# Remainders of expert weights on GpSimd in the second top-k, and another spread of the early expert blocks

## The chip, the cores and the metric

The kernel runs on one NeuronCore of a Trainium2 chip. A core has five engines with a queue of their own each: TensorE (PE, whose weight loads the profile shows apart as PEld), VectorE (DVE), ScalarE (ACT), GpSimd (POOL) and SyncE (SP, which only issues DMAs here). Each works its queue in order, and engines wait for one another by semaphores. The metric is the device time of one execution in microseconds, as the median of several runs.

## The reference

One layer of a hybrid encoder over 1024 tokens of 1024 numbers in float32: a norm, a projection into attention and recurrent parts, their mix, and then the PEER layer, which the change is about:

```
q      = (rmsnorm(h) @ w_query) as (T, 8 heads, 2 halves, 128)
s1, s2 = q[:, :, 0] . sub_keys_1,  q[:, :, 1] . sub_keys_2       # 128 scores each
v1, i1 = top_k(s1, 16);  v2, i2 = top_k(s2, 16)
sc, ci = top_k(v1[..., :, None] + v2[..., None, :], 16)          # the second top-k, of 256 sums
eid    = i1[ci // 16] * 128 + i2[ci % 16];  g = softmax(sc)
act    = gelu(expert_down[eid] . x)
out    = sum over 8 * 16 slots of g * act * expert_up[eid]       # out of 16384 experts
```

followed by a residual sum and a last norm.

## The kernel before, in words

**Two ways through the experts.** The first 3 blocks of 128 tokens fetch their experts' rows one slot at a time by indirect DMA (`gathered`, L875 to L916): 768 steps, each a gather issued on GpSimd (L879) and one long VectorE instruction (L896 or L906) that consumes the row. Five row buffers go round, so a gather waits until VectorE has consumed an earlier row. These steps are strewn through all later stages by `gather_steps`. The other 5 blocks (`ND` = 5, 640 tokens) go the dense way: for each of 128 expert blocks e of 128 experts the product of all their down vectors with all 640 tokens is formed (`down_all`), passed through a GELU, multiplied with a sparse weight matrix that comes from one-hots of the top-k's keys, and multiplied with the up vectors.

**float32 products.** A weight tile is split into a float32r part, cast by ScalarE (`hi`, L126), and the remainder, a subtraction (`lo`, L127). Three products follow each time (`mm3`, L158, L161, L162): hi*hi, hi*lo of the tokens, lo*hi. In `down_all` the tiles are named `draw` (as loaded), `dh`, `dl`; the third product (L162) is the first that needs `dl`. `dh` and `dl` have two buffers, each half an expert block (512 columns). A block is 48 matmuls of 320 columns.

**Early expert blocks.** Of the 128 down products, 71 are formed ahead of the up stage, while other engines prepare the dense weights. `early_downs(n)` adds n to a running sum and forms a block for each whole unit of it; results go to DRAM (`act_d`), all but one. It is called in three loops, with E_QRY / 16 per step of the second query projection (16 steps), E_TOPK / 5 per dense token block in the second top-k, E_OH / 40 per step of the one-hot stage (40 steps of 16 tokens), and after the last step for all that are left.

**The second top-k** (loop over b of 5 token blocks). Nearly all of it is VectorE work: candidate sums, maxima with their indices, softmax, and the keys of the 16 best from comparisons. Its results (`five`) are transposed on TensorE (`ptk`, L1090) one loop step later. No gather steps are added in it (G_TOPK = 0).

**The one-hot stage.** Each step makes three one-hot tiles for 16 tokens (two VectorE instructions, 16 on ScalarE), 48 small matmuls (L1160), and copies of their results to DRAM (`gw_d`); 168 gather steps are spread over it. Then the up stage loads these weights (`gw`), the stored GELUs (`ga`), and forms the remaining down products between the up products.

**The order of the work.** Nobody writes the queues by hand: a planner simulates the program in time and puts each engine's instructions in the order in which they could start, the earlier in the program first. So one-hots appear among the last top-ks, and where an instruction moves to another engine all queues are planned anew. `keep_in_program_order` pins an instruction against the other pinned ones of its engine: the first matmul of each early block, the long VectorE instructions of the gather steps.

Of the kernel before, what the change touches and what calls it, by code (L numbers as in the profile page):

```python
# [39 lines left out]
ND = NT - NG  # L40
# [11 lines left out]
G_UP = 2 * NG * SLOTS - (G_ATT + G_OUT + G_QRY + G_TOPK + G_OH)  # L52
B_OUT, B_CHAIN, B_TURN, B_QRY, B_TOPK = 0, 3, 8, 8, 12
A_STEPS, A_AHEAD, A_FILL, LRU_AT, WO_AT = 3, 4, 0.5, 0.7, 50
E_QRY, E_TOPK, E_OH = 8, 20, 40
TURN5 = 2
OH_LAST = 96
NORM_IN = ((0,), (1,), (2, 3))
# [45 lines left out]
def trunk(  # L104
# [6 lines left out]
    V, A, G, T = nc.vector, nc.scalar, nc.gpsimd, nc.tensor  # L111
# [12 lines left out]
    def split(src, hi, lo, eng=None):  # L124

        A.copy(hi, src)  # L126
        (eng or V).tensor_sub(lo, src, hi.bitcast(F32))  # L127
# [28 lines left out]
    def mm3(ps, wh, wl, mh, ml, first, last, pin=False):  # L156

        t = T.matmul(ps, wh, mh, start=first, stop=False)  # L158
        if pin:
            tc.keep_in_program_order(t)  # L160
        T.matmul(ps, wh, ml, start=False, stop=False)  # L161
        T.matmul(ps, wl, mh, start=False, stop=last)  # L162
# [183 lines left out]
    pin = False  # L346
# [417 lines left out]
    with tc.tile_pool(name="at_gk", bufs=2, side="right") as at_k, \  # L764
# [47 lines left out]
        pin = True  # L812
# [108 lines left out]
    def gather_steps(n):  # L921

        due[0] += n
        while due[0] >= 1.0 - 1e-6:
            due[0] -= 1.0
            next(steps, None)
# [49 lines left out]
    with tc.tile_pool(name="op_d", bufs=1) as op, \  # L976
            tc.tile_pool(name="ps_od", bufs=3, space=PSUM) as ps_a:
        def turn(i, hg, diag):
            for q in range(2):
                pt = ps_t.tile([P, 4, P], F32, name="pt")  # L980
                sl = (slice(None), slice(4 * q, 4 * q + 4), slice(i * P, (i + 1) * P))
                for j in range(4):
                    t = T.matmul(pt[:, j, :], hg[:, (4 * q + j) * P:(4 * q + j + 1) * P], diag,
                                 start=True, stop=True)
                    if j == 0:
                        tc.keep_in_program_order(t)
                split(pt, xH[sl], xL[sl])
# [36 lines left out]
    dp = ctx.enter_context(tc.tile_pool(name="dp", bufs=2))  # L1024
    ps_d = ctx.enter_context(tc.tile_pool(name="ps_d", bufs=3, space=PSUM))

    def down_all(e, pin=False):

        ga = dp.tile([P, TD], F32, name="ga", bufs=2 + HOLD + PRE)
        pd = [ps_d.tile([P, 512], F32, name="pd") for _ in range(2)]  # L1030
        raw = dp.tile([P, KD, P], F32, name="draw", bufs=RAWS)
        nc.sync.dma_start(raw, down_t[e])
        for kh in range(2):
            wh = dp.tile([P, 4, P], F32R, name="dh")
            wl = dp.tile([P, 4, P], F32R, name="dl")
            split(raw[:, 4 * kh:4 * kh + 4, :], wh, wl)
            for c in range(2):
                sl = slice(c * HT, (c + 1) * HT)
                for k in range(4):
                    mm3(pd[c][:, :HT], wh[:, k, :], wl[:, k, :], xH[:, 4 * kh + k, sl],  # L1040
                        xL[:, 4 * kh + k, sl], kh == 0 and k == 0, kh == 1 and k == 3,
                        pin and kh == 0 and c == 0 and k == 0)
        for c in range(2):
            A.activation(ga[:, c * HT:(c + 1) * HT], pd[c][:, :HT], AF.Gelu_apprx_tanh)
        return ga
# [7 lines left out]
    with ExitStack() as ph:  # L1053
        todo = iter(early)
        left = [0.0]

        def early_downs(n):
            left[0] += n
            while left[0] >= 1.0 - 1e-6:
                left[0] -= 1.0  # L1060
                e = next(todo, None)
                if e is None:
                    return
                ga = down_all(e, pin=True)
                if e < HOLD:
                    made[e] = ga
                    continue
                act_d[e] = dram.tile([P, TD], F32, name=f"act{e}")
                nc.scalar.dma_start(act_d[e], ga)
# [4 lines left out]
        with tc.tile_pool(name="qp_d", bufs=3) as qp, \  # L1074
                tc.tile_pool(name="ps_q", bufs=3, space=PSUM) as ps_m, \
                tc.tile_pool(name="ps_qs", bufs=2, space=PSUM) as ps_s:
            for ct, _ in enumerate(query(weights, xH, xL, ND, v12, i12, qp, ps_m, ps_s)):
                if ct in TOPK_AT:
                    top_k_g(1 + TOPK_AT.index(ct), tk, v12_g, i12_g)
                gather_steps(G_QRY / (2 * PH))  # L1080
                early_downs(E_QRY / (2 * PH))
# [13 lines left out]

        last = None
        for b in range(ND):
            early_downs(E_TOPK / ND)

            five = sl_pool.tile([P, 5, P], BF, name="five", bufs=2)  # L1100
            gate = tk.tile([P, PH, TOPK], F32, name="gate_d")
            top_k(v12[:, b], i12[:, b], tk, five[:, 1, :].rearrange("p (h r) -> p h r", h=PH),
                  five[:, 0, :].rearrange("p (h r) -> p h r", h=PH), gate)
            gate = gate.rearrange("p h r -> p (h r)")
            for i in range(2, 5):
                A.copy(five[:, i, :], gate)
                if i < 4:
                    V.tensor_sub(gate, gate, five[:, i, :])
            if last:
                turn(*last)  # L1110
            last = b, five
            gather_steps(G_TOPK / ND)
# [57 lines left out]
        for t0 in range(0, TD, TB):  # L1170
            now = one_hots(t0)
            if t0 == TURN5 * TB:
                turn(*last_five)
            early_downs(E_OH * TB / TD)
            if last:
                weights(*last)
            last = t0, *now
            gather_steps(G_OH * TB / (TD - OH_LAST) if t0 < TD - OH_LAST else 0)
# [6 lines left out]
    with ExitStack() as ph:  # L1185
# [7 lines left out]
        def weigh(e):  # L1193

            if e % EQ == 0:
                gws[e // EQ] = gw = gp.tile([P, TD // TG, EQ * TG], F32, name="gw")
                part, k = (gw_d[0], e) if e < E_FIRST else (gw_d[1], e - E_FIRST)
                nc.sync.dma_start(gw, part[:, :, k:k + EQ, :].rearrange("a p e t -> p a (e t)"))
            gw = gws[e // EQ]
            if e in made:  # L1200
                ga = made[e]
            elif e in act_d:
                ga = dp.tile([P, TD], F32, name="ga", bufs=2 + HOLD + PRE)
                nc.sync.dma_start(ga, act_d[e])
            else:
                ga = down_all(e)
            j = e % EQ
            gv = ga.rearrange("p (a t) -> p a t", t=TG)
            V.tensor_tensor(gv, gv, gw[:, :, j * TG:(j + 1) * TG], op=ALU.mult)
            wh = wp.tile([P, TD], F32R, name="w_h")  # L1210
            wl = wp.tile([P, TD], F32R, name="w_l")
            split(ga, wh, wl)
            ws[e] = (wh, wl)

        for e in range(EARLY, min(EG, EARLY + PRE)):
            made[e] = down_all(e, pin=True)
# [5 lines left out]
        for g in range(NK // EG):  # L1222
            for second in range(2):
# [5 lines left out]
                for j in range(EG):  # L1229
                    e = g * EG + j  # L1230
# [6 lines left out]
                    raw = raw2[:, j % 2, :]  # L1237
# [10 lines left out]
                    wh, wl = ws[e]  # L1248
# [7 lines left out]
                for b in range(ND if end else 0):  # L1256
                    bs = slice(b * P, (b + 1) * P)
                    for e, uh, ul in tail:
                        wh, wl = ws[e]
# [66 lines left out]
```

## Time and profile before

| what | us |
|---|---|
| median of 3 runs (2752.73 to 2758.27) | 2756.99 |
| the profiled execution | 2756.29 |
| its span, first to last instruction | 2754.5 |
| TensorE busy | 2626.9 |
| VectorE busy | 2276.4 |
| ScalarE busy | 1200.6 |
| GpSimd busy | 1042.8 |

Times in the views are microseconds from the start of the span. The second query projection with its early blocks runs from about 685 to 846, the second top-k from there to about 1005, the one-hot stage to about 1410, the up stage to the end. Matmuls are pipelined: each is shown with some 0.31 us for 320 columns but they start closer together, so their pace is read from their starts. An engine's idle time counts only where the work that ends last stands behind it.

### The profile page before, as it was taken

Reading aid. Unit: us, or ns where it says so; the run is one execution under the profiler, and the core shown is the slowest. Engines: PE = TensorE matmul, PEld = TensorE weight load, DVE = VectorE, ACT = ScalarE, POOL = GpSimd, SP = SyncE. Lnnn points to the kernel's source line nnn. Section 1 sums busy time; section 2 is a strip of 40 time slices with the busy share of each in tenths; the row PEclk is TensorE's granted clock in tenths of the full one; section 3 lists DMA queues with packets and bytes.
Section 4 is the critical chain, followed back from the end, with each engine's and each line's share of the span. In section 5 each row is a group of like instructions: output and inputs, shape, how many; then the busy total and the mean of one; then the engine's idle time right before and its main releaser. Section 6 shows DMA issues by size and latency. Waiting matters only on the chain.

```text
span 2754.5 us, 43406 instructions
## 1 busy us (share of the span) xinstructions
PE 2626.9 (95%) x15577; PEld 2323.2 (84%) x15577; DVE 2276.4 (83%) x4737; ACT 1200.6 (44%) x2551; POOL 1042.8 (38%) x850
## 2 busy tenths in 40 slices
PE   7989987889999899999999999999999999999996
PEld 6767965747999899999988888888888888888885
DVE  6565878877999978989967789888888888888897
ACT  5763436722324667888853223222223222222222
POOL 1000223353322015443323445444454545545563
PEclk9999988989999999999999999999999999999998
DMA  5446888877675249999999999999999999999986
GB/s 193 154 138 230 314 242 238 259 256 271 233 255 174 92 162 350 356 341 335 338 370 326 334 351 326 336 332 352 339 332 336 330 340 326 348 338 338 338 288 242
DMA packets 319273, 795.75 MB, mean 289 GB/s; under 512 B 26209, under 2 KB 126577, under 8 KB 316497
## 3 DMA queue, kind: packets, MB, share of 16 engines
q0 software_dynamic: 118128, 428.28, 44.2%
q1 hardware_dynamic: 184112, 297.97, 32.1%
q10 hardware_dynamic: 16816, 66.72, 6.0%
q8 instruction: 122, 2.00, 0.3%
q14 instruction: 95, 0.77, 0.1%
HBM read 690.77 MB, written 102.11 MB: 288 GB/s over the span
## 4 chain that ended last, share of the span: by engine, by line
PE 70%; issue 11%; DMA 9%; DVE 6%; POOL 2%; ACT 2%; SPq 0%; DVEq 0%; ACTq 0%; POOLq 0%
PE pu L158 9%; PE pu L161 9%; PE pu L162 9%; PE pd L162 8%; PE pd L158 8%; PE pd L161 8%; PE pg L1160 4%; PE pa L158 3%; PE pa L162 2%; PE pa L161 2%; POOL row L879 2%; DMA row<-in_expert_up,eid 2%; DMA row<-in_expert_down,eid 2%; DVE row L896 1%; PE pa L606 1%
## 5 line engine op out<-in xcount | busy, mean ns | idle before, releaser
L879 POOL DMA_INDIRECT row<-in_expert_up,eid x384 | 513.1, 1336 | 666.9 <-DVE accg L906 542.2
L879 POOL DMA_INDIRECT row<-in_expert_down,eid x384 | 487.9, 1271 | 631.0 <-DVE row L896 504.2
L158 PE MATMUL pd<-xdH,dh 128*128 128x320 f32 x2048 | 639.6, 313 | 6.0 <-ACT dh L126 3.8
L162 PE MATMUL pd<-xdH,dl 128*128 128x320 f32 x2048 | 631.3, 311 | 10.8 <-DVE dl L127 10.8
L161 PE MATMUL pd<-xdL,dh 128*128 128x320 f32 x2048 | 634.6, 310 | 0.0
L906 DVE SCALAR_TENSOR_TENSOR accg<-row,wg,accg 128x1024 f32<-128x1024 f32 x384 | 491.3, 1279 | 27.0 <-DMA row<-in_expert_up,eid 24.1
L161 PE MATMUL pu<-ul,w_h 128*128 128x512 f32 x1280 | 503.5, 393 | 2.5 <-DVE ul L127 2.5
L162 PE MATMUL pu<-uh,w_l 128*128 128x512 f32 x1280 | 499.6, 392 | 0.0
L896 DVE SCALAR_TENSOR_TENSOR row<-row,x2g 128x1024 f32<-128x1024 f32 x384 | 460.6, 1218 | 32.3 <-DMA row<-in_expert_down,eid 29.9
L162 PEld LDWEIGHTS pd<-xdH,dl 128*128 128x128 f32 x2048 | 385.4, 189 | 19.4 <-DVE dl L127 12.8
L158 PE MATMUL pu<-uh,w_h 128*128 128x512 f32 x1280 | 393.5, 394 | 8.3 <-DVE acc L1261 3.3
L158 PEld LDWEIGHTS pd<-xdH,dh 128*128 128x128 f32 x2048 | 387.0, 189 | 14.5 <-ACT dh L126 4.1
L161 PEld LDWEIGHTS pd<-xdL,dh 128*128 128x128 f32 x2048 | 386.8, 189 | 8.2
L126 ACT CAST uh<-uraw 128x512 fp32r<-128x512 f32 x256 | 157.9, 620 | 498.3 <-PE pu L162 397.5
L161 PEld LDWEIGHTS pu<-ul,w_h 128*128 128x128 f32 x1280 | 241.9, 189 | 50.3 <-DVE ul L127 3.7
L158 PEld LDWEIGHTS pu<-uh,w_h 128*128 128x128 f32 x1280 | 238.1, 189 | 52.5 <-issue 3.7
L162 PEld LDWEIGHTS pu<-uh,w_l 128*128 128x128 f32 x1280 | 241.3, 189 | 47.8
L126 ACT CAST dh<-draw 128x512 fp32r<-128x512 f32 x256 | 157.9, 618 | 241.5 <-PE pd L161 226.9
L127 DVE TENSOR_TENSOR ul<-uraw,uh 128x512 fp32r<-128x512 f32 x256 | 175.5, 687 | 77.6 <-ACT uh L126 76.7
L127 DVE TENSOR_TENSOR dl<-draw,dh 128x512 fp32r<-128x512 f32 x256 | 175.4, 687 | 67.3 <-ACT dh L126 65.2
L126 ACT CAST w_h<-ga 128x640 fp32r<-128x640 f32 x128 | 93.3, 729 | 243.1 <-PE pu L161 166.3
L1147 ACT ACTIVATE o1a<-o,slot_a 128x128 bf16<-128x128 bf16 x640 | 194.1, 428 | 1.8 <-DVE o L1136 1.8
(282 smaller groups left out, 4050.7 us busy)
## 6 DMA issues: line engine op xcount, KB each, us to landing
draw<-in_down_t SPq DMA_DIRECT2D x128, 512.0 KB, 7.0
uraw<-in_up_h SPq DMA_DIRECT2D x128, 512.0 KB, 7.2
gw<-gw_d SPq DMA_DIRECT2D x32, 1280.0 KB, 15.2
gw_d<-st ACTq DMA_DIRECT2D x20, 1536.0 KB, 10.4
act<-ga ACTq DMA_DIRECT2D x70, 320.0 KB, 4.9
ga<-act SPq DMA_DIRECT2D x70, 320.0 KB, 9.7
w_d<-w POOLq DMA_DIRECT2D x32, 512.0 KB, 5.1
w<-w_d SPq DMA_DIRECT2D x32, 512.0 KB, 5.5
```

Of the source, the lines that this page charges most:

```text
L126: A.copy(hi, src)
L127: (eng or V).tensor_sub(lo, src, hi.bitcast(F32))
L158: t = T.matmul(ps, wh, mh, start=first, stop=False)
L161: T.matmul(ps, wh, ml, start=False, stop=False)
L162: T.matmul(ps, wl, mh, start=False, stop=last)
L606: T.matmul(pss[:, t - t0, :], qt[:, t * P:(t + 1) * P], kt[:, ct % 2, :], start=True, stop=True)
L879: nc.gpsimd.indirect_dma_start(out=r, out_offset=None, in_=table, in_offset=bass.IndirectOffsetOnAxis(ap=eids[tb][:, s:s + 1], axis=0))
L896: tc.keep_in_program_order(V.scalar_tensor_tensor(r, r, 1.0, x2, op0=ALU.mult, op1=ALU.mult, accum_out=act[:, s:s + 1]))
L906: tc.keep_in_program_order(V.scalar_tensor_tensor(acc, r, w[:, s:s + 1], acc, op0=ALU.mult, op1=ALU.add))
L1147: A.activation(oa[:, g, :, j], o[:, g, 1, :, j], AF.Copy, scale=slot_a[b][:, tt + t:tt + t + 1])
L1160: T.matmul(ps[:, t - t4, :], o[:, g, 0, :, j], part[:, g, :, j], start=i == 0, stop=i == 2)
```

## The change

In the loop of the second top-k, `early_downs` is called with GpSimd as the engine that forms the remainders `dl` of the weights; in the other loops and in the up stage VectorE goes on forming them. The engine is handed on through `early_downs` and `down_all` to `split`, which could already take one. E_TOPK goes from 20 to 25 (5 and not 4 blocks per token block), E_OH from 40 to 36 (0.9 and not 1 per step). E_QRY stays at 8.

```
@@ -52,7 +52,7 @@
 G_UP = 2 * NG * SLOTS - (G_ATT + G_OUT + G_QRY + G_TOPK + G_OH)
 B_OUT, B_CHAIN, B_TURN, B_QRY, B_TOPK = 0, 3, 8, 8, 12
 A_STEPS, A_AHEAD, A_FILL, LRU_AT, WO_AT = 3, 4, 0.5, 0.7, 50
-E_QRY, E_TOPK, E_OH = 8, 20, 40
+E_QRY, E_TOPK, E_OH = 8, 25, 36
 TURN5 = 2
 OH_LAST = 96
 NORM_IN = ((0,), (1,), (2, 3))
@@ -1024,7 +1024,7 @@
     dp = ctx.enter_context(tc.tile_pool(name="dp", bufs=2))
     ps_d = ctx.enter_context(tc.tile_pool(name="ps_d", bufs=3, space=PSUM))
 
-    def down_all(e, pin=False):
+    def down_all(e, pin=False, eng=None):
 
         ga = dp.tile([P, TD], F32, name="ga", bufs=2 + HOLD + PRE)
         pd = [ps_d.tile([P, 512], F32, name="pd") for _ in range(2)]
@@ -1033,7 +1033,7 @@
         for kh in range(2):
             wh = dp.tile([P, 4, P], F32R, name="dh")
             wl = dp.tile([P, 4, P], F32R, name="dl")
-            split(raw[:, 4 * kh:4 * kh + 4, :], wh, wl)
+            split(raw[:, 4 * kh:4 * kh + 4, :], wh, wl, eng)
             for c in range(2):
                 sl = slice(c * HT, (c + 1) * HT)
                 for k in range(4):
@@ -1054,14 +1054,14 @@
         todo = iter(early)
         left = [0.0]
 
-        def early_downs(n):
+        def early_downs(n, eng=None):
             left[0] += n
             while left[0] >= 1.0 - 1e-6:
                 left[0] -= 1.0
                 e = next(todo, None)
                 if e is None:
                     return
-                ga = down_all(e, pin=True)
+                ga = down_all(e, pin=True, eng=eng)
                 if e < HOLD:
                     made[e] = ga
                     continue
@@ -1095,7 +1095,7 @@
 
         last = None
         for b in range(ND):
-            early_downs(E_TOPK / ND)
+            early_downs(E_TOPK / ND, G)
 
             five = sl_pool.tile([P, 5, P], BF, name="five", bufs=2)
             gate = tk.tile([P, PH, TOPK], F32, name="gate_d")
```

## Rows read from the trace of the kernel before

**Rows 1.** The page, busy time, share and instructions of each engine

```profile
PE 2626.9 (95%) x15577; PEld 2323.2 (84%) x15577; DVE 2276.4 (83%) x4737; ACT 1200.6 (44%) x2551; POOL 1042.8 (38%) x850
```

**Rows 2.** Table by stretch, core 0: PE, PEld, DVE, ACT, POOL busy; PEclk, DMA, GB/s

```profile
846.00:915.00 69.00, 58.90 (x395) 57.55 (x394) 68.97 (x352) 33.09 (x60) 12.97 (x9) 0.97 0.53 181
850.00:1010.00 160.00, 145.74 (x1009) 142.36 (x1008) 146.05 (x586) 95.04 (x190) 13.21 (x10) 0.97 0.39 132
1010.00:1410.00 400.00, 397.45 (x3812) 391.65 (x3810) 353.84 (x304) 336.17 (x918) 173.83 (x116) 1.00 0.92 339
1100.00:1125.00 25.00, 25.00 (x229) 24.70 (x229) 23.43 (x25) 22.59 (x66) 12.81 (x8) 1.00 0.99 371
```

**Rows 3.** Waits of TensorE from 846 to 1010: us, times, longest

```profile
PE ptk L1090 <- DVE cand L670: 6.2, 1, 6.2
PE pd L162 <- DVE dl L127: 5.9, 4, 2.3
PE pd L158 <- ACT ga L1044: 2.2, 2, 1.8
```

**Rows 4.** Timeline of TensorE: start, us, what, [idle before it, releaser]

```profile
853.60 0.31 PE L161 MATMUL pd<-xdL,dh 128*128 128x320 f32 x1
855.16 0.42 PE L162 MATMUL pd<-xdH,dl 128*128 128x320 f32 x1 [1.25 <-DVE dl L127]
...
914.71 0.47 PE L161 MATMUL pd<-xdL,dh 128*128 128x320 f32 x1
...
918.17 0.37 PE L162 MATMUL pd<-xdH,dl 128*128 128x320 f32 x1
```

**Rows 5.** Timeline of ScalarE, two casts of half a block

```profile
849.69 0.62 ACT L126 CAST dh<-draw 128x512 fp32r<-128x512 f32 x1 [2.80 <-PE pd L161]
...
853.21 0.62 ACT L126 CAST dh<-draw 128x512 fp32r<-128x512 f32 x1 [0.88 <-PE pd L161]
```

**Rows 6.** VectorE's instruction groups, 850 to 1010: busy us, mean ns, idle before

```profile
L127 DVE TENSOR_TENSOR dl<-draw,dh 128x512 fp32r<-128x512 f32 x38 | 26.0, 686 | 10.1 <-ACT dh L126 10.1
```

**Rows 7.** The page, DMA issues: count, KB each, us to landing

```profile
draw<-in_down_t SPq DMA_DIRECT2D x128, 512.0 KB, 7.0
...
act<-ga ACTq DMA_DIRECT2D x70, 320.0 KB, 4.9
```

**Rows 8.** GpSimd's instruction groups over the whole span

```profile
masks.py:199 POOL TENSOR_SCALAR_AFFINE_SELECT ident<-ident 128x128 f32<-128x128 f32 x1 | 0.3, 330 | 0.1
```

**Rows 9.** Timeline of GpSimd from 864 to 1017

```profile
864.17 1.68 POOL L879 DMA_INDIRECT row<-in_expert_up,eid  x1 [26.52 <-DVE row L896]
866.16 0.94 POOL L879 DMA_INDIRECT row<-in_expert_up,eid  x1 [0.30 <-issue]
...
886.48 1.75 POOL L879 DMA_INDIRECT row<-in_expert_up,eid  x1 [1.61 <-DMA act<-ga]
940.04 0.24 POOL L1119 IOTA key_f<- 128x128 f32 x1 [51.82 <-ACT ib L688]
1016.78 1.87 POOL L879 DMA_INDIRECT row<-in_expert_up,eid  x1 [76.50 <-DVE accg L906]
```

**Rows 10.** Timeline of VectorE from 844 to 863

```profile
844.86 0.68 DVE L127 TENSOR_TENSOR dl<-draw,dh 128x512 fp32r<-128x512 f32 x1
...
860.29 0.68 DVE L127 TENSOR_TENSOR dl<-draw,dh 128x512 fp32r<-128x512 f32 x1
...
862.66 1.23 DVE L896 SCALAR_TENSOR_TENSOR row<-row,x2g 128x1024 f32<-128x1024 f32 x1
```

**Rows 11.** Waits of VectorE in the one-hot stage, 1010 to 1425

```profile
DVE o1v L1140 <- PE pg L1160: 13.6, 22, 1.5
...
DVE accg L906 <- DMA row<-in_expert_up,eid: 7.1, 3, 3.0
```

**Rows 12.** Table by stretch around the end of the one-hot stage, columns as above

```profile
1407.40:1428.90 21.50, 21.49 (x150) 21.22 (x147) 11.41 (x12) 6.33 (x13) 5.61 (x5) 1.00 1.02 418
1428.90:1447.80 18.90, 12.81 (x73) 12.41 (x74) 7.61 (x16) 4.58 (x8) 0.00 (x0) 0.90 1.08 354
```

More of the change, by code (lines that the diff above doesn't have):

```diff
@@ L54 @@
 A_STEPS, A_AHEAD, A_FILL, LRU_AT, WO_AT = 3, 4, 0.5, 0.7, 50
-E_QRY, E_TOPK, E_OH = 8, 20, 40
+E_QRY, E_TOPK, E_OH = 8, 25, 36
 TURN5 = 2
@@ L1025, in trunk, with down_all @@
     ps_d = ctx.enter_context(tc.tile_pool(name="ps_d", bufs=3, space=PSUM))
-    def down_all(e, pin=False):
+    def down_all(e, pin=False, eng=None):
         ga = dp.tile([P, TD], F32, name="ga", bufs=2 + HOLD + PRE)
@@ L1035, in down_all @@
             wl = dp.tile([P, 4, P], F32R, name="dl")
-            split(raw[:, 4 * kh:4 * kh + 4, :], wh, wl)
+            split(raw[:, 4 * kh:4 * kh + 4, :], wh, wl, eng)
             for c in range(2):
@@ L1055, in trunk, with early_downs @@
         left = [0.0]
-        def early_downs(n):
+        def early_downs(n, eng=None):
             left[0] += n
@@ L1063, in early_downs @@
                     return
-                ga = down_all(e, pin=True)
+                ga = down_all(e, pin=True, eng=eng)
                 if e < HOLD:
@@ L1097, in trunk @@
         for b in range(ND):
-            early_downs(E_TOPK / ND)
+            early_downs(E_TOPK / ND, G)
             five = sl_pool.tile([P, 5, P], BF, name="five", bufs=2)
```

## The prediction

> **What bounds the kernel now.** The page's busy line comes first: TensorE is busy for 95% of the span [rows 1]. Idle time of TensorE is thus nearly all that an edit which leaves its work alone can win, and the question is where that idle time lies. The table by stretch shows it around the change [rows 2]. The stretch with the second top-k (850 to 1010 us) has 145.7 us busy of 160, so 14.3 us idle, at a mean granted clock of 0.97. The one-hot stage after it (1010 to 1410) has 397.4 of 400 at full clock. VectorE is busy 146.0 of 160 in the top-k stretch, and without a pause in its first part: 68.97 of 69 us up to 915 [rows 2].
>
> The waits of TensorE in the top-k stretch add up to the same 14.3 us [rows 3]: one wait of 6.2 us by the transposes `ptk` for the last VectorE result of a top-k, four waits (5.9 us) of the matmuls at L162 for a remainder `dl`, two (2.2 us) for the GELU `ga`. After the long wait matmuls start 0.267 us apart until 918 [rows 4], and not 0.147 as in a stretch without waits (3.52 us from one half block's cast to the next, over 24 matmuls [rows 5]): the lower of the two clock levels, reached after TensorE had stood idle. Over 14 matmuls it costs 14 x 0.12 = 1.7 us more. The same follows the pair of waits at 945 to 949, over 11 matmuls, 1.3 us. So the idle and slow time in this stage is 14.3 + 1.7 + 1.3 = 17.3 us, the most the change can win there.
>
> **The price of one expert block.** It is 48 matmuls (2 halves of K, 2 column halves, 4 k, 3 products) x 0.147 us = 7.05 us of TensorE, two casts of 0.62 us on ScalarE [rows 5], two remainders of 0.685 us on VectorE [rows 6], and 512 + 320 KB of DMA [rows 7].
>
> **The change part by part.** All 71 early blocks remain. Before, 8 + 20 + 40 are given out in the three loops and 3 at the final call; now 8 + 25 + 36, and 2. Five blocks move into the top-k stage: four out of the one-hot stage (its steps 0, 10, 20 and 30 have none, by 0.9 per step), one out of the final call. TensorE's total work is the same; 5 x 7.05 = 35 us of it moves. The top-k stretch grows by 35 us less what it loses in waits, the one-hot stage should shrink by 28, the tail by 7. The end moves only by the change in idle time.
>
> *The wait for a top-k result (6.2 us, and 1.7 at the low clock).* The first `ptk` transposes stand behind the blocks of two top-ks, 8 blocks before, 10 now. That is 2 x 7.05 = 14.1 us of matmuls more ahead of them, over twice the wait, even if VectorE gets no faster at all. From the second top-k on, VectorE has 35 us of matmuls beside each top-k. Without the 26 us of `dl` [rows 6] it has 120 us of the stretch's work left, under 24 per top-k. I take the 7.9 us as gone.
>
> *The remainders (5.9 us).* The 50 `dl` of these 25 blocks leave VectorE for GpSimd. TensorE waited for them because VectorE was behind with other work. What a `dl` may take is read from one that was late: its cast ended at 849.69 + 0.62 = 850.31, and the next matmul, due at 853.60 + 0.15 = 853.75, began at 855.16 [rows 4, 5]. So a remainder has 3.4 us from its cast on. The trace shows no two-input operation on GpSimd. From below, it costs what VectorE takes, 0.685 us. From above, the only GpSimd operation that reads a tile, an affine select of 128 columns, takes 0.330 us [rows 8]: times four for 512 columns is 1.32, and times two for the second input 2.64. I take 1.3, nearest to that row, and both ends lie under 3.4, so by duration alone none is late and the 5.9 us go.
> [...]
>
> *GpSimd's queue.* It is in order and also issues the gathers. At the start of the stage one gather sits at its head for 26.5 us, from 837.65 to 864.17, until VectorE frees a row, and eight more follow until 888, of 0.93 to 2.58 us and 1.4 in the mean, five of them behind a VectorE wait of 0.8 to 2.4, 1.8 in the mean [rows 9]. After that the queue holds nothing but an iota (behind a wait that ends at 940) and the first gather of the one-hot stage (it waits until 1016). On VectorE, five `dl` of the stage's first three blocks (844.86 to 860.29) stood ahead of the operation at 862.66 that releases the 26.5 us gather [rows 10], so I expect the planner to put those of the first blocks ahead of it too. Of the remainders in 864 to 888 some seven fall between gathers. Each has 3.4 - 1.3 = 2.1 us to spare, and a gather with its wait takes 1.4 + 1.8 = 3.2. So some 1.1 us may be lost, for three of the seven: 3 us. Bounds: 0, and 18 us if the first block's remainders stand behind the 26.5 us wait.
>
> *The waits for `ga` (2.2 us, and 1.3 of slow clock)* stand behind other work of ScalarE, of which the change takes nothing away. I leave them.
>
> *The one-hot stage.* Shorter by 28 us, it keeps its one-hots and gathers. VectorE: 353.8 less 8 x 0.685 is 348 of 372 us, 94% (88% now). DMA: 0.92 x 400 = 368 us less 4 x 0.85 MB at 368 MB/ms (339 GB/s over 0.92), 9 us, is 359 of 372, 0.96 [rows 2, 7]. Both have been as high in single stretches with TensorE full (23.4 of 25 and 0.99 at 1100 to 1125) [rows 2]. The skipped blocks ask for the next one-hots 7 us sooner, and VectorE already waits there for a free buffer (13.6 us in all) [rows 11]. I take 0; bounds 0 and 15 (VectorE held at 90%: 348 / 0.9 = 387 us).
>
> *The tail.* The last three blocks cover 1407.4 to 1428.9. Then TensorE is busy 12.8 of 18.9 us while the weights of the experts come back from DRAM, at a DMA share of 1.0 and more [rows 12]. With one block less the cover is 7 us shorter, but the loads stand on SP behind loads that the same blocks release, so most of the gap moves along. I take 2 us lost, bounds -2 and 7.
>
> Sum: -7.9 - 5.9 + 3 + 0 + 2 = -8.8 us. The profiled execution took 2756.3 us (span 2754.5 and 1.8 around it), so 2747.5; the median of the runs is 0.7 above that execution, so I forecast 2748 us.
>
> **The rivals.**
> 1. *GpSimd's queue holds the remainders up (slower).* The place is the gather's 26.5 us wait [rows 9], or those for the iota and the next gather. If the planner puts the first block's remainders behind it, TensorE stands from about 847 to 865, 18 us, and the later gathers cost 1.1 us on all seven, 8 us. With 2 lost in the tail: -13.8 + 18 + 8 + 2 = +14, 2771; with half of it 2758. It decides from 12 us of such waits. For it: the queue is in order and the gathers follow a VectorE that is 100% busy there. Against it: five remainders stood ahead of the releasing operation on VectorE.
> 2. *A remainder on GpSimd takes longer than 3.4 us (slower).* Every half block then waits for the difference: at 3.9 us, 50 x 0.5 = 25 us, so -7.9 + 25 + 2 = +19, 2776; it turns to slower from 3.5. For it: nothing here shows such an operation beside a busy VectorE. Against: the upper bound 2.64.
> 3. *The two engines exclude each other (no change).* Where a GpSimd operation that reads and a VectorE operation with two inputs cannot run at once, each remainder adds its 1.3 us to VectorE when that has such an operation: up to 50 x 1.3 = 65 on 120 us, 185 us, against a stage of 146 + 35 = 181. VectorE would bound the stage again and 4 us more plus the 5.9 us of late remainders would stay: -13.8 + 9.9 + 2 = -2, 2755. No row shows the two together. [...]
> 4. *The one-hot stage does not shrink by 28 us (no change).* VectorE and DMA, at 94% and 0.96, hold it at 379 to 387 us: 7 to 15 us back, 2755 to 2763. For it: early in that stage VectorE already waits for gathered rows [rows 11]. Against: later it does not.
>
> **How the numbers follow.** The forecast has 0.50, with a range of its own from 2739 (all of the 17.3 us) to 2752. The first rival has 0.13, the second 0.08, the third 0.13, the fourth 0.16. A measurement of this kernel can tell about 0.2%, 5.5 us, from no change. Faster comes from the forecast and a little of the third: 0.52. Within 0.2%: most of the third and fourth, and the mild end of the first: 0.28. Slower: the rest, 0.20. From 2737 to 2768 leaves out the second rival and the hard end of the first, and a little at the lower end, 2 in 10.
>
> **What would show it.** In the profile after: no wait of `ptk` for VectorE in this stage; `dl` on GpSimd at about 1.3 us (under 2.64); TensorE's waits for `dl` there at some 3 us; the stage longer by about 20 us and the one-hot stage by 28 shorter with TensorE still at 99%. It is wrong if GpSimd's remainders last over 3.4 us, if a gather ahead of them keeps TensorE waiting over 12 us, if VectorE's operations become longer beside them, or if TensorE gets new waits after the stage.

## The result: slower by 25 us

The changed kernel takes 2782.57 us in the median of 4 runs (2781.79 to 2786.09), the kernel before 2757.63 in runs beside it. The ratio is 1.0097 (95% interval 1.0081 to 1.0114). 2748 was forecast, from 2737 to 2768. The profiled execution of the changed kernel took 2781.8 us, with a span of 2780.0 against 2754.5: 25.5 us more.

**The profile after.** The page's busy line, as [rows 1]:

```profile
PE 2638.2 (95%) x15577; PEld 2332.5 (84%) x15577; DVE 2275.7 (82%) x4687; ACT 1199.7 (43%) x2551; POOL 1109.5 (40%) x900
```

VectorE has 50 instructions fewer, 34 us by [rows 6], and is yet as busy as before. TensorE, with the same matmuls, is busy 11 us longer, so it ran longer at the lower clock, granted at 0.50 for instance from 1152 to 1158 us (mean granted clock 0.976 against 0.980). The table by stretch, as [rows 2, 12] (PE, PEld, DVE, ACT, POOL busy; PEclk, DMA, GB/s), over top-k stage, one-hot stage, tail:

```profile
847.70:1057.00 209.30, 193.26 (x1334) 186.43 (x1334) 165.82 (x568) 113.68 (x239) 92.59 (x63) 0.97 0.43 143
1057.00:1442.00 385.00, 371.62 (x3542) 365.28 (x3541) 345.98 (x295) 318.38 (x873) 170.55 (x116) 0.98 0.91 338
1442.00:1481.20 39.20, 24.97 (x173) 24.70 (x170) 14.60 (x27) 8.87 (x17) 7.43 (x6) 0.84 1.05 393
```

TensorE now stands 16.0 us in the top-k stage and 13.4 in the one-hot stage, which had 2.6 of 400 [rows 2]. Its waits in the top-k stage (840 to 1030), as [rows 3]: us, times, longest:

```profile
PE pd L162 <- POOL dl L127: 9.6, 9, 3.0
PE pd L158 <- ACT ga L1044: 4.0, 2, 2.1
PE pg L1160 <- DVE o1v L1140: 0.8, 1, 0.8
PE pd L158 <- ACT dh L126: 0.7, 1, 0.7
PE ptk L1090 <- DVE five L660: 0.3, 1, 0.3
```

The wait for the top-k result went from 6.2 to 0.3 us, as forecast. In its place stand nine waits for GpSimd's remainders. These as a group (duration min, median, max, then first and last start), answering to [rows 6]:

```profile
L127 POOL TENSOR_TENSOR dl<-draw,dh x50: 1268/1296/3382, 843.9 to 1055.2; 128x512 fp32r<-128x512 f32 x50
```

In the median one takes 1.30 us, the 1.3 that I had taken. The longest of the nine waits, GpSimd and then TensorE:

```profile
957.92 2.76 POOL L879 DMA_INDIRECT row<-in_expert_up,eid  x1 [6.16 <-DVE accg L906]
960.70 1.67 POOL L127 TENSOR_TENSOR dl<-draw,dh 128x512 fp32r<-128x512 f32 x1
```

```profile
962.42 0.42 PE L162 MATMUL pd<-xdH,dl 128*128 128x320 f32 x1 [3.04 <-POOL dl L127]
```

The cast for it had ended at 955.6; the remainder stood behind a gather. Three of the nine waits, 4.8 us, are of this kind: the remainder began 1.2 to 5.1 us after its cast. The other six, also 4.8 us, have remainders that began within 0.1 us of their casts; three of these lasted no more than 1.27 us. And the one-hot products, with what ended TensorE's idle time before them:

```profile
L1160 PE MATMUL pg<-o1v,o x1280: 217/218/312, 956.5 to 1442.0; 128*128 128x128 bf16 x183
...
its engine sat idle before it (us, times) until:
  ACT st L1163: 11.6, 4
```

**Where the 25.5 us lie.** TensorE's loss up to a block is what it took beyond its own work: the time from the stage's first cast to that block's last GELU, less 7.05 us per block and 2.74 per step of weights (48 matmuls x 0.057 us).

| us | before | after |
|---|---|---|
| first cast of the stage, from the start | 841.5 | 843.2 |
| loss up to block 25 of the stage | 29.4 | 35.0 |
| loss up to block 60 | 33.4 | 59.2 |
| from the last weight matmul to the last matmul of all | 1331.5 | 1325.6 |
| from there to the end | 15.4 | 12.1 |

So +1.7 before the stage, +5.6 in the top-k stage, +20.2 in the one-hot stage, +1.2 in the tail and up stage (after the last weights one block fewer is left, so of the difference of -5.9 us 7.05 is the block, and 1.2 is lost), -3.3 at the very end. The first of these is scatter: the first cast comes at 837 to 844 us in the traces below, with no edit ahead of it. The last has a cause: the end comes 10 to 12 us after TensorE's last matmul where the gathered rows are consumed well before it, as in the full change, and some 17 us after the last row where the rows end late (16.8 in e8, 17.5 in the kernel before). In the kernel before it is the row that sets it. The chain that ended last there, around the last row (start, us, what):

```profile
2735.69 1.30 DVE accg L906
2737.01 0.61 ACT row L724
```

The row is consumed at 2737.0 and the end comes 17.5 us behind it, 15.4 behind TensorE's last matmul.

### The profile page after: what moved, and what is told of

It is laid out like the page before. It is cut to its first block, busy times and chain, and to the rows that moved or that the text cites. A ratio compares the mean times of both kernels' runs of the same rounds, so it can differ in the third digit from the quotient of the medians.

```text
span 2780.0 us, 43424 instructions
## 1 busy us (share of the span) xinstructions
PE 2638.2 (95%) x15577; PEld 2332.5 (84%) x15577; DVE 2275.7 (82%) x4687; ACT 1199.7 (43%) x2551; POOL 1109.5 (40%) x900
## 4 chain that ended last, share of the span: by engine, by line
PE 73%; DVE 9%; DMA 8%; issue 6%; ACT 2%; POOL 1%; SPq 0%; POOLq 0%; ACTq 0%; DVEq 0%
PE pu L158 10%; PE pu L161 10%; PE pu L162 10%; PE pd L162 9%; PE pd L158 9%; PE pd L161 9%; PE pg L1160 4%; PE pa L158 2%; PE pa L162 2%; PE pa L161 2%; DMA row<-in_expert_up,eid 2%; DMA row<-in_expert_down,eid 2%; PE pp L158 1%; PE pp L162 1%; PE pp L161 1%
## 5 line engine op out<-in xcount | busy, mean ns | idle before, releaser
L879 POOL DMA_INDIRECT row<-in_expert_down,eid x384 | 481.4, 1254 | 624.2 <-DVE row L896 498.8
L162 PEld LDWEIGHTS pd<-xdH,dl 128*128 128x128 f32 x2048 | 387.1, 190 | 21.8 <-POOL dl L127 12.1
L127 DVE TENSOR_TENSOR dl<-draw,dh 128x512 fp32r<-128x512 f32 x206 | 141.2, 688 | 65.9 <-ACT dh L126 65.2
```

The source lines that it names most:

```text
L879: nc.gpsimd.indirect_dma_start(out=r, out_offset=None, in_=table, in_offset=bass.IndirectOffsetOnAxis(ap=eids[tb][:, s:s + 1], axis=0))
```

## The experiments

All ratios are to the kernel before, in runs on the same chip. Theory S: the spread loses, by the steps of the one-hot stage without a block. Theory G: GpSimd's remainders lose; because a GpSimd instruction that reads and a VectorE instruction with two inputs hold each other up (X), or by GpSimd's queue and the buffers that its work holds (Q). Theory T: with one block fewer behind the last weights the wait for the first up product grows. Theory R: the gathered rows are a second limit. Code is shortened.

**Which half of the change.** Three kernels: only the remainders on GpSimd; only the spread; GpSimd with 21 and 40.

```
e1   -E_QRY, E_TOPK, E_OH = 8, 25, 36   +E_QRY, E_TOPK, E_OH = 8, 20, 40
e2   -early_downs(E_TOPK / ND, G)       +early_downs(E_TOPK / ND)
e3   -E_QRY, E_TOPK, E_OH = 8, 25, 36   +E_QRY, E_TOPK, E_OH = 8, 21, 40
```

> Only the first half of the change: remainders of the second top-k on GpSimd, the blocks spread 20 and 40 as before. Theory S (the spread loses: the three steps of the one-hot stage without an early block leave TensorE to the third weight tile, which ScalarE copies only behind 16 scalings): no step of the one-hot stage is without a block, so the wait of pg for the copy to st (11.3 us after the change) is gone; 2754 to 2762 us, within 0.2% of before. Theory G (the loss is GpSimd's: each remainder takes 1.3 to 3.4 us and holds TensorE and VectorE up in the top-k stage): 2768 to 2776 us, most of the 25 us.

> Only the second half: 25 blocks in the top-k stage and 36 in the one-hot stage, all remainders on VectorE as before. Theory S: the one-hot stage loses as in the full change (pg waits for st some 11 us, and the low clock after each), and VectorE's 50 remainders of 0.69 us, ten more than before, make the top-k stage later still; 2775 to 2788 us. Theory G: the remainders off GpSimd take the loss away; 2750 to 2762 us.

> Remainders on GpSimd, 21 blocks in the top-k stage and 40 in the one-hot stage: no step without a block, and two blocks instead of three left for after the last weights, as in the full change. Against the run with 20 and 40 it tells what the third of those blocks hid. Theory T (with one block fewer the load of the gate weights ends later than the blocks: the wait of the first up product for ScalarE's w_h grows from some 6 to 14 us): 1 to 6 us above the run with 20 and 40, 2757 to 2766 us. Rival (the block only moves to an earlier place): the same time within 1 us.

Measured: GpSimd alone 2764.55 (1.0044, 1.0028 to 1.0060); the spread alone 2758.41 (1.0020, 1.0009 to 1.0031); 21 and 40 2766.04 (1.0043, 1.0031 to 1.0056). Neither theory held whole (the spread alone lies in G's range, GpSimd alone in neither's): GpSimd alone costs some 12 us, the spread 5, and together they cost 25 to 27. Theory T has little for it: e3 and e1 differ by less than their intervals, and the wait of the first up product for `w_h` is 14.0 us in e1, with three blocks, and 15.3 in e3, with two. TensorE's waits in the top-k stage of the spread alone:

```profile
PE pd L162 <- DVE dl L127: 5.8, 3, 2.3
PE pd L158 <- ACT ga L1044: 1.0, 2, 0.6
PE pd L162 <- issue: 0.3, 1, 0.3
```

With the remainders left on VectorE the same 25 blocks cost 7 us of waits, and the loss up to block 25 is 17.5 us: 12 better than before, 17.5 better than with GpSimd. This gain is lost in the full change, which is the likely reason that it costs more than its two halves together. Up to block 60 the loss has grown by 21, much as in the full change (24).

**The steps without a block.** In the full change the stall at one of them: ScalarE (start, us, what), then TensorE (behind it the idle time and what ended it).

```profile
1145.18 1.96 ACT L1163 COPY st<-pg 128x512 f32<-128x512 f32 x3
1147.04 4.82 ACT L1147 ACTIVATE o1a<-o,slot_a 128x128 bf16<-128x128 bf16 x16
1151.73 1.52 ACT L1163 COPY st<-pg 128x512 f32<-128x512 f32 x3
```

```profile
1148.37 0.22 PE L1160 MATMUL pg<-o1a,o 128*128 128x128 bf16 x1
1152.34 0.37 PE L1160 MATMUL pg<-o1v,o 128*128 128x128 bf16 x2 [3.76 <-ACT st L1163]
```

TensorE runs into its three weight tiles in PSUM, since ScalarE's copies, which free them, stand behind 16 scalings. It happens three times, at 1152, 1250 and 1347, ten steps apart. Two kernels change ScalarE's order there: the weights of the step before are given out ahead of the one-hots (e4), and that order is pinned (e5, and e6 with the spread alone).

```
             skipped = left[0] + E_OH * TB / TD < 1.0 - 1e-6
+            if skipped and last:
+                weights(*last)         # e5, e6: the 4 copies and the step's 16 scalings pinned
             now = one_hots(t0)
...
-            if last:
+            if last and not skipped:
```

> The full change, but in a step of the one-hot stage without an early block the weights of the step before are given out ahead of that step's one-hots, so that ScalarE copies them ahead of its 16 scalings. Theory S: the waits of pg for st (11.3 us in three places) and the low clock behind them go; 2762 to 2770 us, 13 to 20 us below the change. Rival (the steps without a block are not the loss, or ScalarE's 4.8 us of scalings are only late in another place, since the next step's weights then wait for the one-hots): 2778 to 2784 us.

> The full change, with ScalarE's order fixed in the steps without a block: first the four copies of the weights of the step before, then the 16 scalings of this step. With the copies only given out earlier, 11 instead of 16 scalings still stood ahead of the first free copy, and each of the three waits went from 3.76 to 2.30 us. Theory S (those waits and the low clock behind them are the spread's loss, some 11.3 us idle and 17 us at the low clock, which is 8.5 us lost): no wait of pg for st over 0.5 us, 14 to 20 us below the full change, 2760 to 2768 us. Rival (they hide another limit of the one-hot stage, VectorE or DMA, which then shows): a new wait in the same places, 2775 to 2782 us.

> The spread alone (25 and 36, all remainders on VectorE), with the same fixed order of copies and scalings. Theory S with X (X: GpSimd's remainders and VectorE's two-input operations exclude each other, which takes the gain of the top-k stage): without either loss the gain of the top-k stage is left, 2740 to 2750 us, faster than before. Rival (VectorE with ten more remainders is the next limit): 2754 to 2760 us.

Measured: 2779.45 (1.0096, 1.0081 to 1.0111), 2780.31 (1.0092, 1.0071 to 1.0114) and 2761.47 (1.0024, 1.0011 to 1.0037). No gain in time. In e4 the planner still put 11 scalings ahead; each wait fell from 3.76 to 2.30 us, by 1.46, which is five scalings of 0.29. So the scalings are what TensorE waits for. TensorE's loss up to block 60 fell by 9 us in e4, and its last matmul ended at 2757.4 instead of 2767.9; but the last gathered row was consumed only at 2757.0, and the end came 17 us after it. So a second limit, which is followed below, hid part of what e4 won on TensorE. Pinning, in turn, moves the wait. In e5, ScalarE at the third of these places:

```profile
1341.35 9.53 ACT L1147 ACTIVATE o1a<-o,slot_a 128x128 bf16<-128x128 bf16 x32 [0.89 <-ACT st L1165]
1350.74 0.74 ACT L1044 ACTIVATE ga<-pd 128x320 f32<-128x320 f32 x2
1351.38 0.57 ACT L1165 COPY st<-pg 128x512 f32<-128x512 f32 x1
```

Now the scalings of two steps come in a row, TensorE waits 2.98 us there, and 2.41 for a late remainder behind it. ScalarE needs 6.8 us for a step without a block (16 scalings in 4.82, four copies of some 0.5), TensorE 2.74: a skipped block takes its casts and GELUs off ScalarE, but none of the step's own work.

Half blocks were to spread the skipping (e11; e12 with the spread alone):

```
-            early_downs(E_OH * TB / TD)
+            early_downs(E_OH * TB / TD, unit=0.5)   # a block's two K halves given out singly
```

> The full change, but in the one-hot stage 0.9 blocks per step are given out in halves, so that eight steps have half a block less and none is without a block. The pinned order told that the copies cannot come earlier, since ScalarE needs 6.8 us per step without a block (16 scalings of 0.30, four copies of 0.49) and TensorE only 2.7. Theory S2 (a step without a block leaves TensorE nothing that covers the other engines' step; half a block does): the waits of pg for st (11.6 us) fall below 4 us and the low clock with them; 2764 to 2772 us. Rival (the stage is short of VectorE's and DMA's time, whatever the grain): the same waits in smaller pieces, 2777 to 2784 us.

> The spread alone (remainders on VectorE) with the same half blocks. Theory S2: the waits of pg for st go from 11.7 us to under 4, 2745 to 2752 us, faster than the kernel before or as fast. Rival: 2756 to 2764 us.

Measured: 2782.17 (1.0113, 1.0097 to 1.0129) and 2755.77 (1.0011, 1.0002 to 1.0020). The waits of pg for st remain at 9.4 and 10.3 us. In e12's trace one matmul of a block stands between two steps at 1264, and the wait of 3.86 follows: the planner gave the halves out early and steps without a block remained. Thus it is not tested whether the stage would shrink if every step gave up a tenth of a block.

The clean test gives every step a block: 76 early blocks instead of 71, 25 of them in the top-k stage, remainders on VectorE (e8).

```
-E_QRY, E_TOPK, E_OH = 8, 20, 40        +E_QRY, E_TOPK, E_OH = 8, 25, 40
-EXTRA = 8                              +EXTRA = 13
```

> The kernel before with 76 instead of 71 early blocks (25 in the top-k stage, 40 in the one-hot stage, 3 after it; five fewer in the up stage), all remainders on VectorE. No step of the one-hot stage is without a block and the tail keeps its three. Theory S: the gain of the top-k stage (its wait of 6.2 us for the top-k result and the slow clock behind it) without the loss of the spread: 2742 to 2752 us. Rival (the five more blocks only cost elsewhere, in VectorE's longer top-k stage and in five more loads of stored GELUs in the up stage): 2755 to 2765 us.

Measured: 2769.98 (1.0056, 1.0039 to 1.0073), so slower, against the expectation. Yet in the one-hot stage TensorE did what theory S says. One row of the table by stretch of e8, one of the spread alone:

```profile
1060.00:1420.00 360.00, 360.00 (x3465) 355.61 (x3462) 327.60 (x282) 309.93 (x851) 156.27 (x105) 1.00 0.93 346
```

```profile
1060.00:1410.00 350.00, 337.28 (x3266) 333.06 (x3265) 322.19 (x273) 303.96 (x844) 167.15 (x103) 0.98 0.93 345
```

With a block in each step TensorE never stops; with 0.9 it stands 12.7 us, and the granted clock is 0.98 besides. The loss from block 25 to 60 is 2.6 us in e8 and 21.0 in the spread alone, so the three skipped steps between cost some 18 us: 6 each, of a block's 7.05. The stage gets shorter by hardly more than 1 us for each block taken out of it.

**The second limit.** Why is e8 slower, with the last matmul at 2718 us (2739 before)? The end of e8 by stretch, and the group of instructions that consume the gathered rows (first and last start behind the durations):

```profile
2650.00:2720.00 70.00, 64.59 (x284) 52.56 (x282) 60.83 (x64) 18.07 (x39) 47.62 (x36) 0.98 0.90 311
2720.00:2750.00 30.00, 0.00 (x0) 0.00 (x0) 23.17 (x19) 0.00 (x0) 21.14 (x16) 0.54 0.89 311
```

```profile
L906 DVE SCALAR_TENSOR_TENSOR accg<-row,wg,accg x384: 1262/1278/1324, 606.4 to 2752.0; 128x1024 f32<-128x1024 f32 x192
```

TensorE is done, and the kernel waits for gathered rows: DMA at 0.89, VectorE at 77%. The last row is consumed at 2753.3 (2737.0 before), the end follows 17 us later. In the kernel before, the last row and TensorE's last matmul are 2.2 us apart. DMA there runs at 0.91 to 0.99 in each 100 us of the up stage but the last, and a longer top-k stage, where it runs at some 0.4, starts the rows later: the row behind the first twenty of the stage is gathered at 1072 us in e8, at 1048 before. The length is not all of it: the spread alone, with the same 25 blocks, gathers it at 1058, because the planner put four rows at 952 to 962 there, and consumes its last row at 2733. Two kernels move 24 gather steps into the last two token blocks of the top-k stage, in e8 (e9) and in the full change (e10):

```
-G_ATT, G_OUT, G_QRY, G_TOPK, G_OH = 64, 24, 46, 0, 168
+G_ATT, G_OUT, G_QRY, G_TOPK, G_OH = 64, 24, 46, 24, 168
-            gather_steps(G_TOPK / ND)
+            gather_steps(G_TOPK / 2 if b >= ND - 2 else 0)
```

> The run with 76 early blocks (25, 40), with 24 of the up stage's gather steps moved into the last two token blocks of the top-k stage. In the run without them TensorE ended at 2718 us, but the last gathered row was consumed only at 2753 and the end came 17 us after that: the row stream starts again some 25 us later (its 20th row of the stage at 1072 against 1048 us) while DMA idles at a share of 0.3 to 0.4, and from then on DMA is at 0.92 to 0.98. Theory R (the row stream is the second limit, and a longer top-k stage delays it): 24 rows earlier bring its end forward by some 20 us or more, 2738 to 2752 us. Rival (VectorE's order, not the stream, sets the end): 2762 to 2772 us, unchanged.

> The full change with the same 24 gather steps in the last two token blocks of the top-k stage. Theory R alone (the change loses because the rows start late: VectorE has no work at 1020 to 1040 us and DMA a share of 0.3): 2757 to 2768 us. Theory S with X (TensorE's own new waits are the bound: it ended at 2768, 10 us after the last row): the rows end earlier but TensorE does not; 2774 to 2784 us.

Measured: e9 2747.26 (0.9977, 0.9966 to 0.9989), some 22 us faster than e8 and faster than the kernel before. e10 2784.16 (1.0112, 1.0096 to 1.0129): no gain, though its last row was consumed 36 us sooner (2722 against 2758); its TensorE ended at 2773.6. So the row stream held e8 back, and the changed kernel is held by TensorE. Its row stream too is 21 us late (2758 against 2737); that would have shown had TensorE not lost more, as it does in e4.

**GpSimd's remainders.** The kernel before, in which GpSimd forms the 40 remainders of the stage once more, unused (e7), and then with two iotas of 512 columns in their place, which read nothing (e13):

```
             split(raw[:, 4 * kh:4 * kh + 4, :], wh, wl)
+            if spare:                                      # e7
+                G.tensor_sub(spare, raw[:, 4 * kh:4 * kh + 4, :], wh.bitcast(F32))
+            if spare:                                      # e13
+                G.tensor_copy(spare[:, :1], wh[:, 0, :1].bitcast(F32))
+                for _ in range(2):
+                    G.iota(spare, pattern=[[1, 4 * P]], base=0, channel_multiplier=0, ...)
```

> The kernel before (20 and 40, remainders on VectorE), to which GpSimd forms each of the 40 remainders of the top-k stage once more into a tile that nobody reads. Theory X (exclusion): VectorE's two-input operations in the stage get longer as in the run with GpSimd's remainders alone (there the same instructions of the stage summed to 162 us, against 142 before), TensorE waits longer for the top-k results; 2758 to 2775 us. Rival Q (the loss comes from waiting for GpSimd's slower result and its queue, so results that nobody reads cost nothing): VectorE's operations as long as before, 2750 to 2757 us.

> The kernel before, with the unused remainders on GpSimd replaced by two iotas of 512 columns each into the same spare tile (behind a copy of one column of the cast, which keeps their place in time): GpSimd is as busy in the same places but reads almost nothing. Theory X (GpSimd's reading and VectorE's two-input operations exclude each other): VectorE's operations as long as before (140 us for those of the top-k, against 151 with the unused remainders), 2751 to 2758 us. Rival Q (GpSimd's queue, or the buffers that its work holds): the loss of the unused remainders stays, 2768 to 2778 us.

Measured: e7 2777.35 (1.0085, 1.0068 to 1.0102), e13 2752.56 (0.9988, 0.9976 to 1.0000). Results that nobody reads cost 22 us; as much GpSimd time that reads but one column costs nothing. The planner's order is not the cause: from the first cast to the last weight matmul TensorE, VectorE and ScalarE run the same instructions in the same order in e7 and e13. Nor are the buffers: in e7 only two loads of `draw` wait for GpSimd's remainders, 4.3 us together, and no cast or matmul does. TensorE waits there for VectorE's own remainders, 24.1 us instead of 5.9:

```profile
PE pd L162 <- DVE dl L127: 24.1, 11, 6.7
```

GpSimd's groups, e7 and then e13:

```profile
L1038 POOL TENSOR_TENSOR spare<-draw,dh x40: 1261/1479/3963, 839.2 to 1028.4; 128x512 fp32r<-128x512 f32 x40
```

```profile
L1041 POOL IOTA spare<- x80: 557/559/583, 843.9 to 1009.3; 128x512 f32 x80
L1039 POOL COPY spare<-dh x40: 183/464/4957, 843.4 to 1006.4; 128x1 f32<-128x1 f32 x40
```

The iotas hardly vary; a copy of a single column takes from 0.18 to 4.96 us. The longest one in e13, GpSimd and then VectorE:

```profile
951.33 4.96 POOL L1039 COPY spare<-dh 128x1 f32<-128x1 f32 x1 [4.54 <-ACT dh L126]
```

```profile
950.82 4.48 DVE L1146 TENSOR_TENSOR o1v<-o,slot_w 128x4096 bf16<-128x4096 bf16 x2
955.22 0.22 DVE L716 TENSOR_TENSOR jb<-wt 128x128 bf16<-128x128 bf16 x1
955.36 0.68 DVE L127 TENSOR_TENSOR dl<-draw,dh 128x512 fp32r<-128x512 f32 x1
955.96 0.28 DVE L717 SCALAR_TENSOR_TENSOR jb<-pb,jb 128x128 bf16<-128x128 bf16 x1
```

The copy began during the first of five VectorE instructions with two inputs, which follow one another without a pause, and ended at 956.29, just behind the fifth (956.24). VectorE's groups from 838 to 1010 (count, busy us, mean ns): the changed kernel, e7, e13.

```profile
L657 DVE TENSOR_TENSOR wt<-wt 128x1024 bf16<-128x1024 bf16 x11 | 11.0, 999 | 0.1
...
L660 DVE TENSOR_TENSOR five<-wt 128x128 bf16<-128x128 bf16 x10 | 5.3, 534 | 0.4
L636 DVE MAX8 sc<-cand 128x8 f32<-128x50 f32 x40 | 5.2, 188 | 0.0
...
L714 DVE TENSOR_TENSOR wt<-wt 128x512 bf16<-128x512 bf16 x6 | 4.6, 768 | 0.1
```

```profile
L127 DVE TENSOR_TENSOR dl<-draw,dh 128x512 fp32r<-128x512 f32 x35 | 30.3, 867 | 1.2 <-ACT dh L126 1.1
...
L636 DVE MAX8 sc<-cand 128x8 f32<-128x50 f32 x40 | 5.2, 187 | 0.0
...
L714 DVE TENSOR_TENSOR wt<-wt 128x512 bf16<-128x512 bf16 x6 | 4.6, 760 | 0.0
```

```profile
L127 DVE TENSOR_TENSOR dl<-draw,dh 128x512 fp32r<-128x512 f32 x40 | 27.1, 680 | 10.4 <-ACT dh L126 10.3
...
L636 DVE MAX8 sc<-cand 128x8 f32<-128x50 f32 x40 | 5.2, 192 | 0.0
...
L714 DVE TENSOR_TENSOR wt<-wt 128x512 bf16<-128x512 bf16 x6 | 2.5, 416 | 0.0
```

Several two-input operations take longer in e7 and the changed kernel (in the mean L714 0.76 and 0.77 us, 0.42 in e13; L660 0.33 and 0.53, 0.22 in e13), L657 in the changed kernel alone (1.00, 0.68 in the other two); the one-input maxima don't (L636 0.19 in all three). The top-k's own instructions sum to 140.6 us on VectorE before, 136.7 in e13, 151.5 in e7, 160.5 with GpSimd alone and 161.8 in the full change. VectorE ends its last top-k 151.0 us after the first cast before and 155.9 with GpSimd alone; with 25 blocks it is 157.7 with the spread alone and 161.6 in the full change. Both times it is later without a single remainder of its own. So these runs bear theory X out: beside GpSimd instructions that read two tiles of 512 columns VectorE's top-k work takes longer (151.5 us in e7), beside iotas, which only write, it does not (136.7 in e13), and GpSimd's own instructions take from 1.26 to 3.96 us in e7. How one engine holds the other is not shown; the copy of one column lasted not for one two-input instruction but for five in a row, 4.96 us, of which the longest takes 2.3.

Do the two losses add up? e9 with its remainders of the top-k stage on GpSimd (e14), where no step is without a block, and e9 tuned once more (e15):

```
e14  -early_downs(E_TOPK / ND)     +early_downs(E_TOPK / ND, G)
e15  -EXTRA = 13   +EXTRA = 14     -G_TOPK = 24   +G_TOPK = 12
```

> The run with 76 early blocks and 24 gather steps in the top-k stage (2747 us), with the remainders of the top-k stage on GpSimd: no step of the one-hot stage is without a block. Theory X, adding up: TensorE loses the 17 us that the same move costs at 25 and 36, all of it in the top-k stage; 2760 to 2768 us. Rival (GpSimd's remainders cost only together with steps that have no block): 2745 to 2752 us.

> The same run with remainders on VectorE, 77 early blocks (the one more goes behind the last weights, where TensorE stood 9.7 us) and 12 instead of 24 gather steps moved (TensorE was the last by 23 us there, so fewer rows need to be early, and DMA is freer when the weights come back). If both hold: 2738 to 2746 us; if the wait behind the last weights is set by the DMA of the weights alone, the block only fills it and 2745 to 2750 us come out.

Measured: e14 2771.59 (1.0068, 1.0053 to 1.0082), 24 us above e9: GpSimd's remainders cost that by themselves, more than the 17 expected (perhaps since the moved rows load VectorE in the same stage; not tested). e15 2755.35 (1.0009, 0.9998 to 1.0019) is slower than e9, against the expectation: its loss grew by 16 us between blocks 30 and 40, where pg waited for st and o1v. The planner put some 14 steps beside these ten blocks, against 8 in e9, so again steps stood without a block. Why it ordered them so was not followed.

## Why the prediction was wrong, step by step

- *The wait for a top-k result.* Right: 6.2 us became 0.3. With the remainders left on VectorE the five more blocks do more than forecast: the loss up to block 25 falls by 12 us.
- *The remainders.* This step failed: "by duration alone none is late and the 5.9 us go", with 3 us for the queue. The 1.3 us was right in the median (1.296), in part by luck: it is the fourfold of a one-input row, without the factor for the second input. The first five remainders did stand ahead of the 26.5 us gather [rows 9], and the queue's 3 us came out as 4 to 5, of which 3.0 stand behind a gather that the planner moved to 958, where the forecast expected none. The 3.4 us that each remainder was given came from one cast; where the cast itself was late only 0.6 to 0.8 were left, and remainders of 1.27 us held TensorE up. Above all, the price of an operation on GpSimd was taken as its own duration alone. What it does to VectorE is of the same size: with 20 blocks VectorE gave up 24.7 us of remainders and got 31 back on the rest (union of its busy time up to the last top-k 147.2 us before, 153.5 with GpSimd alone). Instead of -10.8 us for waits and remainders together the stage gave +5.6: the 12 us gained by the blocks less 17.5 lost by GpSimd.
- *The one-hot stage.* This step failed too, and is the larger: "I take 0", bounds 0 to 15, measured 20.2. It compared VectorE's and DMA's totals with the shortened stage, 94% and 0.96, and took that to fit. The slack is there on average but not at the step that is shortened: the four skipped blocks come ten steps apart, each takes 7 us from one step, and three PSUM tiles and the one-hot buffers carry no such lead. ScalarE was not looked at, and TensorE's wait fell on its copies (3.76 us at 1152). The low clock after each wait (0.50 from 1152 to 1158), also left out, is in the 20.2 (the granted clock of the stage is 0.98, and 1.00 before). Whether VectorE and DMA would have held the stage up had all steps given up the same is open.
- *The tail.* +2 forecast, +1.2 measured with the up stage.
- *"Idle time of TensorE is thus nearly all that an edit which leaves its work alone can win".* This failed as well: in the kernel before, the end follows the last gathered row, while TensorE alone would let it come 3 to 5 us sooner (10 to 12 us after its last matmul). So 8.8 us less on TensorE could win next to nothing with the rows where they were: e8 took 21 us off TensorE's end and came out slower, and with the rows moved (e9) it is faster.
- *The rivals.* The third and the fourth described the two losses, at chances of 0.13 and 0.16, and each alone as no change. The third priced exclusion by VectorE's total against the stage, without the remainders that come late (24.1 us of TensorE's waits in e7); the fourth at 7 to 15 us. They were treated as alternatives, and both happened in the same run. No row read from the kernel before spoke for exclusion or against it.

## What to carry to other kernels

Work that goes from VectorE to GpSimd is priced on both: beside VectorE's instructions with two inputs, operations on GpSimd that read cost VectorE here about as long as they saved it (31 us for 24.7). An unused copy of the work, and as much work that reads nothing, measure this in two runs. Work taken out of a pipelined loop at every tenth step hardly shortened it here, by 1 us of 7: ScalarE still needed its 6.8 us in such a step. Whether the same work taken from every step alike would fare better was not measured. Before costing an edit by the idle time of the busiest engine, look for a second chain that ends with it or sets the end, here the gathered rows, and move both: the version that did (e9) is the fastest of these kernels.

## What the hardware showed unexpectedly

A GpSimd copy of one column lasted up to 4.96 us (0.18 at least) beside VectorE's two-input work, with the same single column each time; the longest one ended only when a row of five such VectorE instructions was over. Conversely a VectorE operation of 128 columns (L660) went from 0.22 to 0.53 us in the mean beside remainders of 1.3.
